# Norm 2's shift and the first low parts move from GpSimd to VectorE, the first gates into a step of their own, the last masks back

## The chip, the cores and the metric

The kernel runs on one core of a Trainium2 chip. The metric is the device time of one execution in microseconds (us). The engines have short names in the profile: PE (TensorE, matrix products and transposes), DVE (VectorE), ACT (ScalarE), POOL (GpSimd), SP (SyncE, which only issues transfers here). PEld is PE's loading of weights.

## What is computed

Two layers over 256 tokens and 256 context tokens of width 1024. Each layer modulates a norm, runs four mixers side by side, adds their output to the residual, norms again, and sends the result through a mixture of 16 experts. What the change touches is the second norm and the experts:

```python
def modulate(h, shift, scale):
    return h * (1.0 + scale) + shift

x = x + gt1 * (jnp.concatenate([ya, yb, ys, yh], axis=-1) @ w_out[l])
h2 = modulate(rms_norm(x, norm2_g[l]), sh2, sc2)
x = x + gt2 * moe(h2, router_w, router_b, moe_w1[l], moe_w3[l], moe_w2[l])
```

`moe` takes the softmax of the 16 router logits, picks the best of four groups of experts by the sum of its two best scores, keeps the two best experts of that group, divides their scores by their sum (the gates), and adds gate times `(silu(h @ w1) * (h @ w3)) @ w2` of these two. Layer 0 does all of this for the context as well; layer 1 for the 256 tokens alone.

## The kernel before

Rows (tokens) lie on the 128 partitions: layer 0 has four tiles of 128 rows in this part, layer 1 two. `wout` multiplies by `w_out`, and for each half of a tile `done` makes the new residual (`yf<-mm,gt`, `yf<-yf,x`). `half` squares and transposes it, `logits` multiplies it by the router's weights, `finish` makes the tile's logits (`lgt`) and the exponentials (`sce`). `norm` writes the tile `x` (it is h2 now): residual times the row's factor (`l21z` and its like, from a few 128x1 operations on DVE) times the scale `a`, plus the shift `sh`. The tile goes to `h2d` in DRAM, by a transfer from SP.

`route` then ranks the scores on DVE: `t<-sce`, `rk`, `og`, `Ab`, then `oh` and `rsrc`, the rows of the first two experts (they have fixed places). `z` is a column of zeros, written at the same point; an operation that takes it as bias can't start earlier. `rri` comes at the end of `route`: it says where each row's entry goes in the table of slots. GpSimd scatters eight times (`sld<-rec,rri`; four in layer 1), and loads the table: `rtab` holds row numbers and gates of all other slots.

The experts run one after another. Their rows are gathered by GpSimd from `h2d` (`xg<-h2d,rsrc` for the first, `xg<-h2d,rtab` later), transposed by PE (`tp<-cst,xg`), and split into a high part and the rest (`ah` on ACT, `al` on DVE). Weights come as 1 MB transfers on SP's queue (`raw<-in_wmoe_dram`), at most three in flight. `split` makes their high part on ACT (`hi<-raw`) and their low part on DVE (`lo<-raw,hi`), 128x1024 at a time, and PE takes three products for each pair: high by high, low by high, high by low (`sc` and `mm` are the PSUM tiles). Small experts (all of layer 1, and those with up to 64 slots in layer 0) run in `expert32` with unsplit weights. Results are multiplied by the gate and scattered to `ybd` in DRAM. In each layer a loop for surplus rows, with a barrier of all engines, stands behind the first two experts (`extras`, L2031); with these inputs it makes no pass. The last expert is added from masks in place of the scatter: `rel` is the row number less the tile's first row, and the masks `ah<-iota_b,rel` compare it with a row of numbers.

The order on each engine is that of the code, as generators are stepped by `moe`, except where a scheduler with a table of costs interleaves. Every operation passes one helper, so the profile gives line 383 for all of them (382 in the changed kernel); they are told apart by their tiles.

Of the kernel before, what the change touches and what calls it, by code (L numbers as in the profile page):

```python
# [15 lines left out]
AF = mybir.ActivationFunctionType  # L16
ALU = mybir.AluOpType
AX = mybir.AxisListType

P = 128  # L20
# [29 lines left out]
KORD = ((4, 5, 6, 7, 2, 3, 0, 1), (0, 1, 6, 7, 4, 5, 2, 3))  # L50
SLOTS = (32, 32)
NPRE = 3
NPP = 3
AHEAD2 = (9, 11)
FLIGHT = 3
STAT = 2
# [333 lines left out]
class Kern:  # L390
# [1165 lines left out]
    def wout(self, l, xsrc):  # L1556
        nc, I = self.nc, self.I
# [9 lines left out]
        for k in KORD[l]:  # L1567
            hi, lo = self.hilo()
# [63 lines left out]
        def norm(i, a):  # L1632
            c = 1 if i < 2 else 0
            h = xt[i]
            last = i == ot[-1]
            for n in range(2):
                s = slice(n * 512, n * 512 + 512)
                nc.vector.scalar_tensor_tensor(h[:, s], self.x2[i][n], rs[i], a2[c][:, s], op0=ALU.mult, op1=ALU.mult)
                if last:
                    (nc.vector if n else nc.gpsimd).tensor_tensor(h[:, s], h[:, s], sh[c][:, s], op=ALU.add)  # L1640
                    nc.sync.dma_start(self.h2d[l][a * P:(a + 1) * P, s], h[:, s])
            if last:
                return
            nc.gpsimd.tensor_tensor(h, h, sh[c], op=ALU.add)
            nc.sync.dma_start(self.h2d[l][a * P:(a + 1) * P, :], h)

        def flush(j):
            i, n, t = later[j]
# [272 lines left out]
    def moe(self, l, route):  # L1921
# [29 lines left out]
        for e in range(NE):  # L1951
            if e == STAT:

                while len(self.pre) < AHEAD2[l]:
                    m, j = USE[self.wi]
                    self.pre.append(self.fetch(source(m)(j)))
                self.extras(l)
            if STAT <= e + 2 < NE:
                for n in both(e + 2):
                    xg[n] = self.gather(l, *sl[n], m=min(P, SLOT[l][e + 2]))  # L1960
            for j in range(2):
                if e or j:
                    next(gens[e])
                if e:
                    next(gens[e - 1], None)
            next(gens[e])
            if e == NE - 1:
                while self.wi < len(USE):
                    self.pre.append(self.fetch(source(USE[self.wi][0])(USE[self.wi][1])))
                self.combine_g2(l)  # L1970
            if e + 1 < NE:
                begin(e + 1)
            next(gens[e])
# [77 lines left out]
    def halves_of(self, wsrc, alone, n):  # L2051

        nc = self.nc
        for j in range(6):
            if not alone:
                raw = self.load(wsrc(j))
            for hf in range(2):
# [5 lines left out]
                        self.splitx(*hl, src[:, q])  # L2063
                        yield hl
                else:
                    hi, lo = self.split(raw[:, c], after=self.zero0 if NPP <= 2 * j + hf < n else None, eng=nc.gpsimd if 2 * j + hf < min(n, NPP) else None)
                    yield hi[:, 0:512], lo[:, 0:512]
                    yield hi[:, 512:1024], lo[:, 512:1024]

    def expert(self, l, wsrc, tiles, m, ahead=0, alone=False):  # L2070
# [50 lines left out]
        for n in range(2):  # L2121
# [5 lines left out]
                    self.mm3(ps[:m], es[i][0][:, t], es[i][1][:, t], hi, lo, k == 0, k == 3)  # L2127
            c = slice(n * 512, n * 512 + 512)
            for i, ps in enumerate(py):
                nc.scalar.activation(ys[i][:m, c], ps[:m], AF.Copy, scale=tiles[i][2][:m])  # L2130
        for y, (_, rows, *_) in zip(ys, tiles):
            self.add_rows(l, y, rows, m)

# [10 lines left out]
    def expert32(self, l, wsrc, tile, m, last=False):  # L2144
# [51 lines left out]
        if G > 1:  # L2196
# [3 lines left out]
                    nc.tensor.matmul(pt[:, o:o + m], lhsT=s[:, k * P:(k + 1) * P], rhs=self.fold, start=True, stop=True)  # L2200
            t = self.act("al", F32)
            nc.scalar.activation(t[:, :4 * m], pt[:, :4 * m], AF.Silu)
            nc.vector.tensor_tensor(h[:, :4 * m], t[:, :4 * m], pt[:, 4 * m:8 * m], op=ALU.mult)
        else:
            nc.vector.tensor_tensor(s1[:m], s1[:m], p3[:m], op=ALU.mult)
            for k in range(4):
# [2 lines left out]
        if last:  # L2209

            self.ohT = self.act("ah", F32R).rearrange("p (a t) -> p a t", t=P)[:m]
            rel = self.s([P, 4], "rel", bufs=1)
            for a in range(NT):
                nc.vector.tensor_scalar(rel[:m, a:a + 1], rows[:m], 1.0 - 128.0 * a, None, op0=ALU.add)
                nc.vector.tensor_scalar(self.ohT[:, a], self.iota_b[:m], rel[:m, a:a + 1], None, op0=ALU.is_equal)
            t = self.ring_tile(F32R)
            yh, yl = self.ylast = t[:m, 0], t[:m, 1]
        yield
# [135 lines left out]
```

## Time and profile before

| | us |
|---|---|
| median of 3 runs | 1307.47 (1305.84 to 1308.94) |
| profiled execution, its own time | 1307.14 |
| its span, first to last instruction | 1305.1 |
| PE, DVE, ACT, POOL busy | 1146.0, 731.1, 529.9, 183.9 |
| granted clock of PE, mean share | 0.931 |

The span is what the views below divide up; the 2.0 us between it and the execution's own time lie outside it. Starts of instructions are counted from the span's begin. Layer 0's second norm and routing take about 360 to 403 us, its experts before the loop 403 to 450; the same in layer 1 is 965 to 1000 and 1000 to 1042.

### The profile page before, as it was taken

The numbers are of one execution on the slowest core, as the hardware profiler recorded it, in microseconds if no ns is written. First come the engines' busy times: TensorE is split into PE (matmuls) and PEld (weight loads), VectorE is DVE, ScalarE is ACT, GpSimd is POOL, SyncE is SP. The second block draws the span as 40 slices with busy tenths as digits, with TensorE's granted clock in tenths as the row PEclk, the third lists the DMA queues.
The fourth block names the chain that finished last, engine by engine and source line by source line (L and its number), as shares of the span: only waits on it lengthen the run. The fifth ranks groups of instructions, "written<-read, shape, count | busy, mean of one in ns | idle before, by whom it ended". The sixth has DMA issues, their size and how long they took to land. (4 is left out here: it accounts for less than half of the span.)

```text
span 1305.1 us, 16882 instructions
## 1 busy us (share of the span) xinstructions
PE 1146.0 (88%) x5789; PEld 724.5 (56%) x5789; DVE 731.1 (56%) x1811; ACT 529.9 (41%) x876; POOL 183.9 (14%) x213
## 2 busy tenths in 40 slices
PE   4999999997966799999898799998884499998885
PEld 2677677765855567655454277684771253533332
DVE  6496579788588564455444659599974110101114
ACT  5222642674324464555434452553831122212222
POOL 0200200100044220211100100100102111211102
PEclk9999999896987799999999899999896789999997
DMA  7763752444817798899995743554477699999961
GB/s 298 261 235 135 257 204 86 177 153 158 350 49 258 238 355 319 313 367 387 384 361 183 279 162 131 201 173 162 149 277 314 242 337 396 365 389 388 414 265 65
DMA packets 62009, 334.05 MB, mean 256 GB/s; under 512 B 12217, under 2 KB 13657, under 8 KB 27104
## 3 DMA queue, kind: packets, MB, share of 16 engines
q1 hardware_dynamic: 51840, 313.44, 63.0%
q0 software_dynamic: 10080, 19.50, 5.8%
q8 instruction: 47, 0.77, 0.2%
q14 instruction: 42, 0.34, 0.1%
HBM read 317.51 MB, written 19.15 MB: 258 GB/s over the span
## 5 line engine op out<-in xcount | busy, mean ns | idle before, releaser
L383 DVE TENSOR_TENSOR lo<-raw,hi 128x1024 fp32r<-128x1024 f32 x169 | 203.5, 1222 | 87.4 <-ACT hi L383 82.9
L383 PE MATMUL sc<-raw,ah 128*64 128x512 f32 (+3 forms) x750 | 216.2, 634 | 12.8 <-SPq L2031 9.5
L383 ACT CAST hi<-raw 128x1024 fp32r<-128x1024 f32 x172 | 175.3, 1047 | 116.5 <-PE mm L383 53.6
L383 PEld LDWEIGHTS sc<-raw,ah 128*64 128x64 f32 (+3 forms) x750 | 62.3, 147 | 113.3 <-issue 99.5
L383 PE MATMUL mm<-hi,ah 128*128 128x512 f32 (+3 forms) x264 | 109.1, 415 | 4.4 <-ACT hi L383 4.3
L383 PE MATMUL mm<-lo,ah 128*128 128x512 f32 (+3 forms) x264 | 107.0, 405 | 1.7 <-DVE lo L383 1.6
L383 PE MATMUL mm<-hi,al 128*128 128x512 f32 (+3 forms) x264 | 105.7, 402 | 0.6 <-DVE al L383 0.6
L383 PE MATMUL mm<-raw,ah 128*64 128x512 f32 (+3 forms) x378 | 100.2, 595 | 1.9 <-DVE ah L383 1.9
L383 PE MATMUL mm<-ah,hi 128*128 128x512 f32 (+1 forms) x224 | 88.4, 399 | 1.1 <-DVE ah L383 0.8
L383 PE MATMUL sc<-hi,ah 128*128 128x512 f32 (+3 forms) x176 | 75.8, 432 | 11.5 <-ACT hi L383 6.8
L383 DVE COPY al<-sc 128x512 f32<-128x512 f32 x21 | 14.5, 690 | 126.8 <-PE sc L383 126.8
L383 PE MATMUL mm<-al,hi 128*128 128x512 f32 (+1 forms) x224 | 83.8, 374 | 0.0
L383 PE MATMUL mm<-ah,lo 128*128 128x512 f32 (+1 forms) x224 | 83.2, 372 | 0.0
L383 PE MATMUL ad<-raw,cT 128*32 128x256 f32 (+1 forms) x512 | 67.7, 530 | 11.3 <-DMA raw<-in_wada_dram 8.5
L383 DVE TENSOR_TENSOR s<-s,mm 64x512 f32<-64x512 f32 (+1 forms) x43 | 29.2, 678 | 85.1 <-ACT s L383 85.1
L383 PE MATMUL sc<-lo,ah 128*128 128x512 f32 (+3 forms) x176 | 73.2, 416 | 2.1 <-DVE lo L383 2.1
L383 PE MATMUL sc<-hi,al 128*128 128x512 f32 (+3 forms) x176 | 72.1, 410 | 0.0
L383 PEld LDWEIGHTS tp<-fold,al 128*128 128x128 f32 x336 | 43.0, 201 | 48.9 <-DVE al L383 23.9
L383 PE MATMUL tp<-fold,al 128*128 128x64 f32 x336 | 46.9, 289 | 23.8 <-DVE al L383 14.9
L383 PEld LDWEIGHTS mm<-hi,ah 128*128 128x128 f32 (+3 forms) x264 | 49.4, 188 | 28.3 <-ACT hi L383 6.4
L383 PEld LDWEIGHTS mm<-raw,ah 128*64 128x64 f32 (+3 forms) x378 | 32.7, 142 | 58.3 <-issue 52.0
L383 ACT ACTIVATE al<-tp 128x256 f32<-128x256 f32 x21 | 8.1, 384 | 130.1 <-PE tp L383 130.1
(432 smaller groups left out, 2037.0 us busy)
## 6 DMA issues: line engine op xcount, KB each, us to landing
raw<-in_wmoe_dram SPq DMA_DIRECT2D x192, 1024.0 KB
raw<-in_wada_dram SPq DMA_DIRECT2D x32, 1024.0 KB
raw<-in_win_dram SPq DMA_DIRECT2D x24, 1024.0 KB
raw<-in_wad_dram SPq DMA_DIRECT2D x16, 1024.0 KB
raw<-in_wout_dram SPq DMA_DIRECT2D x8, 1024.0 KB
x<-in_tok_dram SPq DMA_DIRECT2D x8, 512.0 KB
raw<-ybd SPq DMA_DIRECT2D x6, 512.0 KB
slot<-yf SPq DMA_DIRECT2D x36, 64.0 KB
```

The source lines that it names most:

```text
L383: r = f(*a, **k)
```

## The change

1. `norm`: the shift is added by DVE, half a tile (128x512) right behind the multiply of that half. Before, GpSimd added it, 128x1024 at a time, apart from the last tile of a layer, of which GpSimd added the first half and DVE the second.
2. `halves_of`: in layer 0 the first expert's first three low parts were made on GpSimd, and their high parts on ACT waited for nothing but their weights. Now they are made on DVE like all others, and the first three high parts wait for `z` (`after=self.zero0`).
3. `expert`: with `ahead` (the first expert of layer 0) the two halves of the result are copied out of PSUM without the gate, and a multiply of the whole row by the gate follows in a step of the generator of its own. `moe` has one more step for it.
4. `expert32(last)`: the instructions of `rel` and of the masks are ordered behind the product `h`. Before, the masks' operands alone put them in order.

```diff
-NPP = 3
...
                 nc.vector.scalar_tensor_tensor(h[:, s], self.x2[i][n], rs[i], a2[c][:, s], op0=ALU.mult, op1=ALU.mult)
+                nc.vector.tensor_tensor(h[:, s], h[:, s], sh[c][:, s], op=ALU.add)
                 if last:
-                    (nc.vector if n else nc.gpsimd).tensor_tensor(h[:, s], h[:, s], sh[c][:, s], op=ALU.add)
                     nc.sync.dma_start(self.h2d[l][a * P:(a + 1) * P, s], h[:, s])
-            if last:
-                return
-            nc.gpsimd.tensor_tensor(h, h, sh[c], op=ALU.add)
-            nc.sync.dma_start(self.h2d[l][a * P:(a + 1) * P, :], h)
+            if not last:
+                nc.sync.dma_start(self.h2d[l][a * P:(a + 1) * P, :], h)
...
             next(gens[e])
+            if e:
+                next(gens[e - 1], None)
...
-                    hi, lo = self.split(raw[:, c], after=self.zero0 if NPP <= 2 * j + hf < n else None, eng=nc.gpsimd if 2 * j + hf < min(n, NPP) else None)
+                    hi, lo = self.split(raw[:, c], after=self.zero0 if 2 * j + hf < n else None)
...
-                nc.scalar.activation(ys[i][:m, c], ps[:m], AF.Copy, scale=tiles[i][2][:m])
+                if ahead:
+                    nc.scalar.copy(ys[i][:m, c], ps[:m])
+                else:
+                    nc.scalar.activation(ys[i][:m, c], ps[:m], AF.Copy, scale=tiles[i][2][:m])
+        if ahead:
+
+            yield
+            for y, (_, _, gate) in zip(ys, tiles):
+                nc.scalar.activation(y[:m], y[:m], AF.Copy, scale=gate[:m])
...
-            nc.vector.tensor_tensor(h[:, :4 * m], t[:, :4 * m], pt[:, 4 * m:8 * m], op=ALU.mult)
+            i = nc.vector.tensor_tensor(h[:, :4 * m], t[:, :4 * m], pt[:, 4 * m:8 * m], op=ALU.mult)
...
-            for a in range(NT):
-                nc.vector.tensor_scalar(rel[:m, a:a + 1], rows[:m], 1.0 - 128.0 * a, None, op0=ALU.add)
-                nc.vector.tensor_scalar(self.ohT[:, a], self.iota_b[:m], rel[:m, a:a + 1], None, op0=ALU.is_equal)
+            with self.tc.issue_after(i.ins):
+                for a in range(NT):
+                    nc.vector.tensor_scalar(rel[:m, a:a + 1], rows[:m], 1.0 - 128.0 * a, None, op0=ALU.add)
+                    nc.vector.tensor_scalar(self.ohT[:, a], self.iota_b[:m], rel[:m, a:a + 1], None, op0=ALU.is_equal)
```

The order of DVE's instructions at the end of layer 0's routing, before, around `rri` (`rr` and `rXT` are its last steps, `al_3810` and `al_3819`, the first expert's, stand 18 and 16 rows ahead of it):

```order
L383 TENSOR_REDUCE rXT_3742<-rov_3740 128x4
L383 SCALAR_TENSOR_TENSOR rr_3758<-rXT_3742 128x8
L383 TENSOR_TENSOR lo_3856<-raw_3085,hi_3855 128x1024
L383 SCALAR_TENSOR_TENSOR rr_3758<-rq_3757,rr_3758 128x8
L383 TENSOR_TENSOR lo_3866<-raw_3085,hi_3865 128x1024
L383 TENSOR_SCALAR rri_3764<-rr_3758 128x8
```

And now, on DVE, from ahead of the first `al` (a third low part, `lo_3796`, stands 21 rows higher, behind `z`) and then up to `rri`:

```order
L382 TENSOR_TENSOR lo_3800<-raw_3081,hi_3799 128x1024
L382 TENSOR_REDUCE rXT_3745<-rw_3749 128x4
L382 TENSOR_TENSOR lo_3804<-raw_3083,hi_3803 128x1024
L382 TENSOR_TENSOR rw_3749<-ru_3744,o_773_3689 128x64
L382 TENSOR_TENSOR al_3813<-tp_3807,ah_3812 128x512
```

```order
L382 TENSOR_TENSOR lo_3859<-raw_3085,hi_3858 128x1024
L382 TENSOR_REDUCE rXT_3745<-rov_3743 128x4
L382 TENSOR_TENSOR lo_3869<-raw_3085,hi_3868 128x1024
L382 TENSOR_TENSOR rov_3743<-ru_3744,o_773_3689 128x64
L382 TENSOR_TENSOR lo_3897<-raw_3087,hi_3896 128x1024
L382 TENSOR_REDUCE rXT_3745<-rov_3743 128x4
L382 TENSOR_TENSOR lo_3907<-raw_3087,hi_3906 128x1024
L382 SCALAR_TENSOR_TENSOR rr_3761<-rXT_3745 128x8
L382 SCALAR_TENSOR_TENSOR rr_3761<-rq_3760,rr_3761 128x8
L382 TENSOR_SCALAR rri_3767<-rr_3761 128x8
```

Three low parts have come ahead of the first `al`. Between `z` and `rri` there are now eight (`lo_3848`, not shown, is the fourth), where there were two.

The order of ACT at the end of expert 0, where its result `y` leaves PSUM, before and now (`hi` are the next expert's high parts; the second half's `y` stood two `hi` further down before):

```order
L383 CAST hi_3997<-raw_3270 128x1024
L383 ACTIVATE y_3949<-mm_3950,rtab_3790 128x512
L383 CAST hi_4007<-raw_3270 128x1024
L383 CAST hi_4020<-raw_855_4018 128x1024
```

```order
L382 CAST hi_3997<-raw_3270 128x1024
L382 COPY y_3952<-mm_3953 128x512
L382 CAST hi_4007<-raw_3270 128x1024
L382 CAST hi_4020<-raw_855_4018 128x1024
L382 COPY y_3952<-mm_3975 128x512
L382 CAST hi_4030<-raw_855_4018 128x1024
L382 ACTIVATE y_3952<-y_3952,rtab_3793 128x1024
L382 CAST hi_4074<-raw_866_4072 128x1024
```

The instruction that reads `rtab` has moved behind three more high parts.

The order of DVE at the end of layer 1's routing, before and now (`al<-sc` and `ah` are an `expert32`'s):

```order
L383 TENSOR_SCALAR rri_9064<-rr_9060 128x4
L383 TENSOR_SCALAR rel_10696<-rtab_9078 64x1 x2
L383 COPY al_9124<-sc_9092 128x512
L383 TENSOR_TENSOR ah_9134<-al_9144,tp_9135 128x256
L383 TENSOR_TENSOR s_1996_9154<-s_1996_9154,mm_9149 64x512
```

```order
L382 TENSOR_SCALAR rri_9069<-rr_9065 128x4
L382 COPY al_9129<-sc_9097 128x512
L382 TENSOR_TENSOR ah_9139<-al_9149,tp_9140 128x256
L382 TENSOR_TENSOR s_1996_9159<-s_1996_9159,mm_9154 64x512
```

`rel`, which reads `rtab`, has left this place; it now stands directly ahead of the masks of the last expert, in layer 0 (four) as in layer 1 (two).

## Rows read from the trace of the kernel before

**Rows 1.** The page: the span, and each engine's busy time, share and instructions.

```profile
span 1305.1 us, 16882 instructions
...
PE 1146.0 (88%) x5789; PEld 724.5 (56%) x5789; DVE 731.1 (56%) x1811; ACT 529.9 (41%) x876; POOL 183.9 (14%) x213
```

**Rows 2.** Table by stage: length, engines' busy time (instructions), granted clock, DMA share, GB/s.

```profile
core 0: us, PE busy (x) PEld busy (x) DVE busy (x) ACT busy (x) POOL busy (x), PEclk, DMA share, GB/s
360.00:403.00 43.00, 20.72 (x125) 17.96 (x124) 38.22 (x116) 9.45 (x22) 21.67 (x12) 0.72 0.16 58
403.00:431.00 28.00, 26.53 (x110) 20.79 (x110) 20.46 (x42) 15.68 (x18) 11.45 (x9) 0.89 0.93 351
985.00:1000.00 15.00, 1.84 (x16) 1.45 (x16) 6.23 (x44) 0.50 (x1) 3.96 (x4) 0.50 0.59 234
1060.00:1260.00 200.00, 188.51 (x848) 80.68 (x844) 25.88 (x42) 46.78 (x82) 27.00 (x22) 0.97 1.01 391
```

**Rows 3.** PE's timeline, where it starts again behind each layer's barrier: start, duration, operation, [idle].

```profile
449.63 0.80 PE L383 MATMUL sc<-hi,ah 128*128 128x512 f32 x1 [4.72 <-issue]
...
1042.00 1.98 PE L383 MATMUL sc<-raw,ah 128*64 128x512 f32 x4 [9.50 <-SPq L2031]
```

**Rows 4.** GpSimd's timeline, layer 0's routing; in brackets idle time before <- releaser.

```profile
365.06 2.82 POOL L383 TENSOR_TENSOR x<-x,sh 128x1024 f32<-128x1024 f32 x1 [29.60 <-DVE x L383]
...
373.57 6.97 POOL L383 TENSOR_TENSOR lo<-raw,hi 128x1024 fp32r<-128x1024 f32 x3 [2.67 <-ACT hi L383]
```

**Rows 5.** VectorE's timeline, the same stage.

```profile
363.50 0.74 DVE L383 SCALAR_TENSOR_TENSOR x<-yf,l20z,a 128x512 f32<-128x512 f32 x1
...
364.90 3.53 DVE L383 SCALAR_TENSOR_TENSOR x<-yf,l21z,a 128x512 f32<-128x512 f32 x2
...
369.09 2.36 DVE L383 TENSOR_TENSOR yf<-yf,x 128x512 f32<-128x512 f32 x1
...
376.00 2.27 DVE L383 SCALAR_TENSOR_TENSOR l22u<-l22z,l22h 128x1 f32<-128x1 f32 x1
...
384.98 1.21 DVE L383 TENSOR_TENSOR lo<-raw,hi 128x1024 fp32r<-128x1024 f32 x1
...
393.33 0.68 DVE L383 TENSOR_TENSOR x<-x,sh 128x512 f32<-128x512 f32 x1
```

**Rows 6.** VectorE's timeline, layer 1's routing.

```profile
994.62 0.16 DVE L383 TENSOR_SCALAR z<-tp 128x1 f32<-128x1 f32 x1 [8.31 <-DMA h2d<-x]
```

**Rows 7.** The first gather and what follows: timelines of GpSimd, PE and VectorE.

```profile
398.57 1.11 POOL L383 DMA_INDIRECT xg<-h2d,rsrc  x1 [4.80 <-DVE rcap L383]
...
403.09 1.94 PE L383 MATMUL tp<-cst,xg 128*128 128x128 f32 x8 [5.57 <-DVE wix L383]
...
404.83 0.69 DVE L383 TENSOR_TENSOR al<-tp,ah 128x512 fp32r<-128x512 f32 x1 [0.33 <-ACT ah L383]
```

**Rows 8.** Layer 0 up to the barrier: timelines of GpSimd, ScalarE and PE.

```profile
412.71 1.90 POOL L383 DMA_INDIRECT sld<-rec,rri  x1 [9.95 <-DVE rri L383]
...
424.42 1.27 POOL L383 DMA_INDIRECT sld<-rec,rri  x1 [0.31 <-issue]
...
435.69 1.63 POOL L383 DMA_INDIRECT ybd<-y,rtab  x1 [0.30 <-DMA xg<-h2d,rtab]
...
442.43 1.05 POOL L383 DMA_INDIRECT xg<-h2d,rtab  x1 [5.12 <-PE tp L383]
...
431.64 0.69 ACT L383 ACTIVATE y<-mm,rtab 128x512 f32<-128x512 f32 x1 [5.59 <-DMA rtab<-sld]
...
433.31 0.80 PE L383 MATMUL sc<-hi,ah 128*128 128x512 f32 x1 [3.13 <-ACT hi L383]
...
441.12 1.03 PE L383 MATMUL tp<-cst,xg 128*128 128x128 f32 x8
```

**Rows 9.** Layer 1 up to the barrier: timelines of VectorE and PE.

```profile
1017.57 0.21 DVE L383 TENSOR_SCALAR rel<-rtab 64x1 f32<-64x1 int32 x2 [15.03 <-DMA rtab<-sld]
...
1017.70 0.67 DVE L383 COPY al<-sc 128x512 f32<-128x512 f32 x1
...
1018.42 1.97 PE L383 MATMUL tp<-fold,al 128*128 128x64 f32 x8 [6.99 <-DVE al L383]
```

**Rows 10.** VectorE's timeline, the end of layer 1.

```profile
1278.03 4.34 DVE L383 TENSOR_SCALAR ah<-iota_b,rel 64x128 fp32r<-64x128 bf16 x2
```

## The prediction

> **What bounds the kernel now.** I read the page first, then a table by stage, then each engine's timeline at the two places that the diff touches, with the waits in it. The page gives TensorE (PE) 1146.0 us of a span of 1305.1, VectorE (DVE) 731.1, GpSimd (POOL) 183.9 [rows 1]. The table shows how little that average says here: in layer 0's routing stage, 360 to 403 us, PE is busy 20.72 of 43 us and DVE 38.22; in 403 to 431 PE has 26.53 of 28; in 1060 to 1260 the DMA share is 1.01 [rows 2]. So DVE sets the pace from 360 to 403, and later what happens on it is mostly covered. Does a gain in that stage survive the stages behind it? I take it that it does: in each layer a loop of zero passes ends with a barrier of all engines, behind which PE starts again at 449.63 and at 1042.00 [rows 3]. Up to there the transfers in flight have landed, so the engines start from the same state however early it is, and the stages bound by PE or by DMA behind it move along. What counts is how far each of the two barriers moves.
>
> **Part 1: the shift on DVE, layer 0.** GpSimd's timeline beside DVE's shows a pattern. While GpSimd adds (2.82 us from 365.06) or makes a low part (three, 6.97 us from 373.57) [rows 4], DVE's operations last until GpSimd is through: a pair of multiplies 3.53 us where one takes 0.74, an add 2.36, a 128x1 operation 2.27 [rows 5] where another takes 0.16 [rows 6]. The excess up to the last tile's logits: the pair 3.53 - 1.48 = 2.05; two adds (one shown) 2 x (2.36 - 0.68) = 3.4; three 128x1 operations (one shown) 3 x 2.1 = 6.3; together 11.75. The low part that DVE itself makes there, 1.21 [rows 5], goes to a later place. New on DVE are halves of the shift, of which one is there today, with 0.68 us [rows 5]; six stand ahead of the last logits, 4.1. DVE idles 43 - 38.22 = 4.8 us in this stage [rows 2], in waits for PE or ScalarE (ACT); I let a third of the new work fall into them, 1.4. Net 11.75 + 1.2 - 4.1 + 1.4 = 10.2. Behind the last logits one more stall goes and one more half comes, about even. So the first gather, issued at 398.57, and PE's transposes of its rows at 403.09 [rows 7] come **10.2 us earlier**. Bounds: 7.6, if the low part's 1.2 and the waits' 1.4 give nothing; below nothing, if it isn't GpSimd that stretches DVE (rival F).
>
> The Trainium skill, "SBUF — State Buffer", section "Who interferes with whom", says that a VectorE instruction with two SBUF inputs and a GpSimd instruction that reads SBUF shut each other out for a whole instruction; the 3.53 and 2.36 us agree, and the 2.27 of an operation on one column as well. By it all of the 11.75 goes and rival F is out.
>
> **Part 2: what DVE does instead.** Expert 0's first low parts are now made on DVE, behind the routing, since their high parts wait for its `z`. The order of DVE shows three of them ahead of the first `al`, which ends today at 404.83 + 0.69 = 405.52 with 0.33 of waiting before it [rows 7]; PE wants it for its third product. 3 x 1.2 - 0.3 = 3.3 us. The four high parts on ACT lie between `z` and the gathered rows, inside the 4.5 us that the gather takes to PE (398.57 to 403.09 [rows 7]): nothing; if that cover were gone, they would cost their length. PE's products of expert 0 move by 10.2 - 3.3 = 6.9.
>
> GpSimd's eight scatters wait for `rri`, 9.95 us until 412.71 [rows 8]. `rri` stood behind two low parts and stands behind eight. Six more cost 7.2 if nothing covers them; 3.3 if they fit into DVE's waits for the high parts and only PE's delay counts. I take 6.3, close to the first, as DVE has few gaps there: `rri`, and with it the table, come 10.2 - 6.3 = **3.9 earlier** (bounds 3.0 and 6.9).
>
> **Part 3: the gate in a step of its own.** Today ACT waits 5.59 us for the table at 431.64 with `y<-mm,rtab`, high parts queue behind it, and PE idles 3.13 until 433.31 [rows 8]. Now three more high parts stand ahead of the multiply that needs the table, and PE can go on. Then come transposes of rows gathered by the table, at 441.12 today [rows 8]. The table is there at 431.6 - 3.9 = 427.7, a gather takes 4.5 to PE, and I allow GpSimd 0.5 to begin it: 432.7, 8.4 earlier. GpSimd's last gather ahead of the barrier, 442.43, waits for those transposes, and the barrier opens 7.2 us behind it (449.63) [rows 3, 8]: 441.2 by this chain. The other is `ybd`, 435.69 today [rows 8]; it keeps its distance of 4.0 from the table, comes at 431.8, and needs no more than the 13.9 that it has to the barrier today: 445.7 at the latest. Between the two I take 442.6, nearer to the first, since `ybd` is not the last to be issued: **-7.0** for layer 0, bounds -3.9 (the table's gain alone) and -10.2 (the first gather's).
>
> **Part 4: the masks held back.** In layer 1 two `rel` wait 15.03 us for the table on DVE until 1017.57. The copy `al<-sc` is queued behind them, and PE waits for it 6.99 us, until 1018.42 [rows 9]. With `rel` gone the copy runs when PE's `sc` is done, and PE goes on at 1011.4. The barrier at 1042.00 [rows 3] moves by **-6.5**, with half a us lost on the way; bounds -7.0 and 0 (rival A). At the end `rel` now stands ahead of the masks: two take 0.21 [rows 9], four in layer 0 twice that, and in layer 1 they stand in a place where DVE is stretched (4.34 for two masks at 1278.03 [rows 10]): **+0.6** in all.
>
> Layer 1's adds and stalls I cost at nothing: at 994.62 DVE waits 8.31 us for the transfer of those very rows [rows 6]; without that cover three halves would cost 2.0.
>
> **Sum.** -7.0 - 6.5 + 0.6 = -12.9. The profiled execution took 1307.14 with its span of 1305.1, and the median of the three is 1307.47; the sum is made against 1307.1: **1294.2 us**, a span of about 1292.
>
> **The rivals.** 0.2% (2.6 us) is about what a measurement of this kernel can tell from no change.
>
> A. Layer 1's wait is hidden anyway. PE's 9.50 us of idle time ahead of 1042.00 end with SyncE's queue [rows 3], which carries the weights; if its last transfers end as today, PE only idles longer. Against it: they wait for buffers that PE frees. 1307.1 - 7.0 + 0.6 = 1300.7. Chance 0.12.
>
> B. The low parts eat layer 0's gain: the gather gains only 7.6, and `rri` loses 7.2 of it; table, gather and barrier keep 0.4. -0.4 - 6.5 + 0.6: 1300.8. For it: `rri` is the head of the longest chain to the barrier. 0.12.
>
> C. GpSimd's scatters stretch with a busier DVE. Eight of them fill 412.71 to 425.69, the first with 1.90 us, the last with 1.27 [rows 8]. At 1.90 and a gap of 0.3 each they would fill 17.6 instead of 13.0: the table 4.6 later, layer 0 -2.4: 1298.8. 0.04. The Trainium skill, "SBUF — State Buffer", in its box on the "DVE blocks DMA" trap, says that a transfer issued by GpSimd waits for its descriptors while VectorE runs in a two-port mode; that speaks against work moved to VectorE, and by it the time would be C's. The scatters' lengths here, unequal beside low parts on DVE, leave it open.
>
> D. All of it counts: the gather's 10.2 and the masks' 7.0. 1307.1 - 17.2 + 0.6 = 1290.5. 0.10.
>
> E. Slower, by PE's clock. Where PE runs in pieces, 985 to 1000, the granted clock is 0.50, its 1.2 GHz; in 403 to 431 it is 0.89 [rows 2]. If low parts made one by one break expert 0's products up so that PE stays at 1.2 GHz through them, 26.53 us become 26.53 x 0.89 / 0.50 = 47.2, 20.7 longer: layer 0's barrier comes 20.7 - 10.2 = 10.5 later, and the sum is 10.5 - 6.5 + 0.6 = +4.6: 1311.7. It decides from 18.7 of these 20.7 on (2.6 over). Against it: 110 products in 26.53 us are 0.24 each, six of them to a low part 1.45, more than the 1.2 that DVE takes. 0.08.
>
> F. Something other than GpSimd stretches DVE, and the change doesn't do what it says. Then seven halves (4.8) and the three low parts (3.3) come on top of today's time; with -7.0 + 0.6 that is +1.7: 1308.8, no change by the bound. 0.06.
>
> **How the numbers follow.** My own case has 0.48; its own range is 1291 to 1299.5, layer 0 between -9.5 and -3.9 and layer 1 between -7.0 and -5. From 1289 to 1302.5 lie A to D too; E and F (0.14) and a few ends of the others are left out. Faster: 0.48 + 0.12 + 0.12 + 0.04 + 0.10 = 0.86. Same: F, 0.06. Slower: E, 0.08.
>
> **What would show it.** Right: no DVE operation of one column over 0.5 us and no pair over 1.6 from 361 to 380; the first gather near 388; the scatters from about 408.5; no wait of PE for a high part behind expert 0; the first barrier near 442.6; in layer 1 `al<-sc` without a wait for the table, and the distance between the barriers 6 to 7 us shorter. Wrong: a gather that moved with a barrier that did not (B); a longer idle time ahead of the second barrier (A); a granted clock near 0.5 in expert 0 (E).

## The result, and the profile after

| | before | changed |
|---|---|---|
| median, first comparison | 1306.65 us (4 runs, 1299.51 to 1308.94) | 1289.55 us (4 runs, 1286.50 to 1294.32) |
| ratio, 95% interval | | 0.9889 (0.9856 to 0.9921) |
| median, second comparison | 1307.27 us (11 runs) | 1293.10 us (6 runs) |
| ratio, 95% interval | | 0.9884 (0.9856 to 0.9913) |
| profiled execution, its own time; span | 1307.14; 1305.1 | 1286.50; 1283.3 |

Faster by 1.1 to 1.2%, some 15 us. (The ratios are the recorded ones, with their intervals; the medians by themselves would give 0.987 and 0.989.) The page after, span and busy times, beside [rows 1]:

```profile
span 1283.3 us, 16883 instructions
...
PE 1135.7 (88%) x5789; PEld 717.1 (56%) x5789; DVE 723.3 (56%) x1824; ACT 531.7 (41%) x877; POOL 162.0 (13%) x204
```

GpSimd has lost 21.9 us, DVE 7.8, although DVE has more instructions (1824 for 1811): it does more and waits less inside its instructions. The timeline of DVE in layer 0's routing, beside [rows 5]:

```profile
358.32 0.74 DVE L382 SCALAR_TENSOR_TENSOR x<-yf,l20z,a 128x512 f32<-128x512 f32 x1
...
359.72 0.75 DVE L382 SCALAR_TENSOR_TENSOR x<-yf,l21z,a 128x512 f32<-128x512 f32 x1
...
362.45 0.68 DVE L382 TENSOR_TENSOR yf<-yf,x 128x512 f32<-128x512 f32 x1
...
367.06 0.22 DVE L382 SCALAR_TENSOR_TENSOR l22u<-l22z,l22h 128x1 f32<-128x1 f32 x1
...
382.18 0.16 DVE L382 TENSOR_SCALAR rsrc<-tp 128x2 int32<-128x2 f32 x1 [0.30 <-PE tp L382]
```

Up to `rsrc` no operation is stretched any more: a single multiply takes 0.75, the add 0.68, the operation of one column 0.22 (2.36 and 2.27 before). The next rows are GpSimd, PE, VectorE and ScalarE from the first gather to the barrier, beside [rows 3, 7, 8]:

```profile
383.18 1.11 POOL L382 DMA_INDIRECT xg<-h2d,rsrc  x1 [13.31 <-DVE rcap L382]
...
384.29 1.87 POOL L382 MEMSET xg<- 128x1024 f32 x2
...
387.53 1.94 PE L382 MATMUL tp<-cst,xg 128*128 128x128 f32 x8 [5.39 <-DMA xg<-h2d,rsrc]
...
392.43 0.80 PE L382 MATMUL sc<-hi,al 128*128 128x512 f32 x1 [1.91 <-DVE al L382]
...
397.14 0.39 PE L382 MATMUL sc<-lo,ah 128*128 128x512 f32 x1
...
384.92 1.28 DVE L382 COPY rat<-cst 128x2 f32<-128x2 f32 x1
...
385.34 1.19 DVE L382 TENSOR_TENSOR lo<-raw,hi 128x1024 fp32r<-128x1024 f32 x1
...
402.50 0.17 DVE L382 TENSOR_SCALAR rri<-rr 128x8 int32<-128x8 f32 x1
...
402.95 1.03 POOL L382 DMA_INDIRECT sld<-rec,rri  x1 [15.50 <-DVE rri L382]
...
419.27 0.61 POOL L382 DMA_DIRECT2D rtab<-sld  x1 [3.87 <-DMA sld<-rec,rri]
...
431.55 1.05 POOL L382 DMA_INDIRECT xg<-h2d,rtab  x1 [1.60 <-PE tp L382]
...
423.96 1.15 ACT L382 ACTIVATE y<-y,rtab 128x1024 f32<-128x1024 f32 x1 [6.43 <-DMA rtab<-sld]
...
429.33 1.94 PE L382 MATMUL tp<-cst,xg 128*128 128x128 f32 x8 [7.93 <-DMA xg<-h2d,rtab]
...
437.71 0.66 PE L382 MATMUL sc<-hi,ah 128*128 128x512 f32 x1 [2.15 <-issue]
```

In layer 1, DVE and PE, beside [rows 3, 6, 9], and the masks at the end, beside [rows 10]:

```profile
981.89 0.16 DVE L382 TENSOR_SCALAR z<-tp 128x1 f32<-128x1 f32 x1 [9.21 <-DMA h2d<-x]
...
997.07 0.69 DVE L382 COPY al<-sc 128x512 f32<-128x512 f32 x1 [7.21 <-PE sc L382]
...
997.81 2.00 PE L382 MATMUL tp<-fold,al 128*128 128x64 f32 x16
...
1014.10 1.08 PE L382 MATMUL tp<-cst,xg 64*128 64x64 f32 x8 [6.37 <-DMA xg<-h2d,rtab]
...
1022.36 1.97 PE L382 MATMUL sc<-raw,ah 128*64 128x512 f32 x4 [3.82 <-SPq L2030]
...
1256.88 0.20 DVE L382 TENSOR_SCALAR rel<-rtab 64x1 f32<-64x1 int32 x2
...
1257.05 3.97 DVE L382 TENSOR_SCALAR ah<-iota_b,rel 64x128 fp32r<-64x128 bf16 x2
```

The reader is to see three things. `al<-sc` waits for PE, not for the table; PE goes from one product to the next there (997.81) and waits later, 6.37 us, for rows gathered by the table. In layer 0 PE has no wait for a high part; it now waits 7.93 us for gathered rows at 429.33. And the starts can't be compared as they stand: the stage itself began 5.18 us earlier (358.32 for 363.50 [rows 5]), ahead of any instruction that the change touches. So all places below are counted from DVE's first `x<-yf,l20z` in layer 0, and in layer 1 from `z<-tp`:

| us | gather (POOL) | `rri` (DVE) | table at ACT | transposes (PE) | barrier 1 (PE) | barrier 1 to `z` | `z` to barrier 2 | from there to the end |
|---|---|---|---|---|---|---|---|---|
| before | 35.07 | 48.76 | 68.14 | 77.62 | 86.13 | 544.99 | 47.38 | 263.08 |
| changed | 24.86 | 44.17 | 65.63 | 71.01 | 79.39 | 544.18 | 40.47 | 260.95 |
| difference | -10.21 | -4.59 | -2.51 | -6.61 | **-6.74** | -0.81 | **-6.91** | -2.13 |

With the 5.18 ahead of it all, the row adds up to the spans' difference of 21.8 us: 5.18 + 6.74 + 0.81 + 6.91 + 2.13. The changed kernel profiled again (e10, below) gave barrier 1 at 79.65 and `z` to barrier 2 in 40.51, but began the stage at 363.89 and had a span of 1292.9. So some 13.5 us come back each time, and the 5.18 did not; they are the spread between executions, which reaches 9 us for one kernel. In the fourteen profiles of this document the stage begins between 358.32 and 364.61, and up to there the instructions of all of them are the same, in the same order.

Barrier 1 has a spread of its own: e12 (below) differs from the changed kernel in layer 1 alone, and its first barrier comes at 77.56. Three profiles with the same instructions up to there thus give 77.56, 79.39 and 79.65, and smaller differences than these 2.1 us, between two profiles, say little about it.

Which engine holds barrier 1? It opens when the last one has come to it. In the kernel before that is VectorE, with a low part that ends at 447.76, 1.87 us ahead of PE's restart:

```profile
446.54 1.22 DVE L383 TENSOR_TENSOR lo<-raw,hi 128x1024 fp32r<-128x1024 f32 x1
```

Now it is ScalarE, with a high part that ends at 436.64, 1.07 ahead of the restart, and two low parts stand behind the barrier:

```profile
435.60 1.04 ACT L382 CAST hi<-raw 128x1024 fp32r<-128x1024 f32 x1 [0.69 <-PE sc L382]
...
438.43 2.36 DVE L382 TENSOR_TENSOR lo<-raw,hi 128x1024 fp32r<-128x1024 f32 x2 [2.14 <-issue]
```

From the stage's begin to the barrier VectorE and GpSimd made 24 low parts before, and VectorE makes 22 now. None of the four parts of the change names this; the order of the code came out so.

The second barrier waits for weights. The table by stage for eight microseconds ahead of it, before and then now (the column ahead of the last is the DMA share):

```profile
core 0: us, PE busy (x) PEld busy (x) DVE busy (x) ACT busy (x) POOL busy (x), PEclk, DMA share, GB/s
1015.00:1023.00 8.00, 4.58 (x16) 2.61 (x17) 1.22 (x4) 0.38 (x1) 1.96 (x2) 0.50 0.34 124
```

```profile
1010.00:1018.00 8.00, 3.90 (x16) 1.69 (x16) 0.00 (x0) 0.58 (x1) 0.07 (x1) 0.58 1.02 334
```

Before, the transfers of weights had a hole behind PE's stop at 1011.43: SyncE's queue waited for PE's `sc` products, which had to free the buffers, 9.4 us at the longest; now it is 2.9, and the DMA share stays at 1.0 until 1018. In both kernels the transfers are through 1.4 to 2 us ahead of PE's restart (the share is 0.00 from 1040 before, and from 1021 now). So what came back in layer 1 is the hole in the transfers, and PE's new wait at 1014.10 costs nothing, as the weights move on during it.

### The profile page after: what moved, and what is told of

It is laid out like the page before. It is cut to its first block, busy times and chain, and to the rows that moved or that the text cites. A ratio compares the mean times of both kernels' runs of the same rounds, so it can differ in the third digit from the quotient of the medians.

```text
span 1283.3 us, 16883 instructions
## 1 busy us (share of the span) xinstructions
PE 1135.7 (88%) x5789; PEld 717.1 (56%) x5789; DVE 723.3 (56%) x1824; ACT 531.7 (41%) x877; POOL 162.0 (13%) x204
## 5 line engine op out<-in xcount | busy, mean ns | idle before, releaser
L382 DVE TENSOR_TENSOR lo<-raw,hi 128x1024 fp32r<-128x1024 f32 x172 | 206.6, 1221 | 85.7 <-ACT hi L382 80.1
L382 ACT CAST hi<-raw 128x1024 fp32r<-128x1024 f32 x169 | 172.2, 1047 | 112.6 <-PE mm L382 52.9
L382 PE MATMUL sc<-raw,ah 128*64 128x512 f32 (+3 forms) x750 | 213.3, 628 | 6.2 <-SPq L2030 3.8
L382 PE MATMUL tp<-cst,xg 64*128 64x64 f32 (+4 forms) x264 | 31.4, 261 | 32.9 <-DMA xg<-h2d,rtab 14.3
```

Source lines behind the costliest of these rows:

```text
L382: r = f(*a, **k)
```

## The experiments

All places are counted as in the table above.

**One part at a time.** Each kernel is the one before with one of the four edits of the diff above; e5 has two of them.

e1, the shift alone:

```diff
+                nc.vector.tensor_tensor(h[:, s], h[:, s], sh[c][:, s], op=ALU.add)
...
-            nc.gpsimd.tensor_tensor(h, h, sh[c], op=ALU.add)
```

> Only the shift moves to VectorE; the three first low parts stay on GpSimd. Counted from VectorE's first x<-yf,l20z in layer 0: rsrc came 34.06 us later before, 23.86 with the whole change. Theory (GpSimd's adds stretch VectorE, each for as long as it runs): the pair, two adds and the t<-sce give back about 6.4, seven halves cost 4.7, GpSimd's low parts still cost 6: rsrc at about 32, first barrier 2 us earlier, layer 1 unchanged, time -2 us. Rival (something else stretches VectorE): the halves come on top, rsrc at 38 to 39, time +4.

e4, the low parts alone:

```diff
-                    hi, lo = self.split(raw[:, c], after=self.zero0 if NPP <= 2 * j + hf < n else None, eng=nc.gpsimd if 2 * j + hf < min(n, NPP) else None)
+                    hi, lo = self.split(raw[:, c], after=self.zero0 if 2 * j + hf < n else None)
```

> Only the three low parts move to VectorE, their high parts behind z; the shift stays on GpSimd. Theory: the three stretched 128x1 operations (6.3) and the low part on VectorE (1.2) go: rsrc at 34.06 - 7 = 27; six low parts more ahead of rri take 5 to 6 of it back: rri at 48.76 - 1 = 47.5, first barrier 0 to 1 us earlier, time the same. Rival (the first gather alone decides): barrier 5 us earlier, time -5.

e2, the masks alone:

```diff
+            with self.tc.issue_after(i.ins):
```

> Only the masks are held back. Theory: layer 1's stretch from z to PE behind the second barrier, 47.38 us before and 40.47 with the whole change, falls to about 40.5 by this part alone; layer 0's first barrier (86.13 after the first x<-yf,l20z) does not move, since ScalarE's gated y still waits for the table there; time -6 us. Rival (the barrier's wait hides it, the gain came from elsewhere): 47 stays and the time is the same.

e3, the gate alone:

```diff
+                if ahead:
+                    nc.scalar.copy(ys[i][:m, c], ps[:m])
...
+        if ahead:
+
+            yield
+            for y, (_, _, gate) in zip(ys, tiles):
+                nc.scalar.activation(y[:m], y[:m], AF.Copy, scale=gate[:m])
```

> Only the gate gets its own step. Theory: ScalarE no longer waits for the table at the first y, but VectorE's rel still does, with low parts queued behind it, so PE still stops for a low part within a few us: first barrier within 1 us of 86.13, time the same. Rival (the gate alone held PE): PE runs on to the transposes, barrier 3 to 4 us earlier, time -3.5.

e5, gate and masks together, both edits as above:

> The gate's own step and the masks held back, together; shift and low parts as before. The gate alone put the first barrier at 88.09 us after the first x<-yf,l20z (86.13 before), the masks alone at 86.16. Theory: each alone only passes the wait for the table to the other engine, both together take it off PE's path; PE's transposes, 77.62 before, come 5 behind the table's 68, at 73, and the barrier at 82; layer 1 as with the masks alone (41.7), time -10 us. Rival (the parts only add): barrier at 88, time -4.

e11, the whole change but the gate:

```diff
-                if ahead:
-                    nc.scalar.copy(ys[i][:m, c], ps[:m])
-                else:
-                    nc.scalar.activation(ys[i][:m, c], ps[:m], AF.Copy, scale=tiles[i][2][:m])
+                nc.scalar.activation(ys[i][:m, c], ps[:m], AF.Copy, scale=tiles[i][2][:m])
```

> The whole change without the gate's own step. Theory (ScalarE's gated y holds three high parts back until the table is there, at about 65.5, and only then come 4.6 us of products or more ahead of the transposes): transposes at 74, first barrier at 82 to 83 instead of 79.4, time 3 us more than the whole change. Rival (PE waits for the table's rows in either order): barrier at 79.4, same time.

e10, the changed kernel again, with no edit:

> The changed kernel itself, for its time in the same call. Theory: ratio to before 0.989, first barrier at 79.4, layer 1's stretch from z to the second barrier at 40.5. Rival (part of the first result, 5 us of which stood ahead of any changed instruction, was chance): ratio 0.992 to 0.993 with the same stretches.

What was measured:

| kernel | `rsrc` | `rri` | table at ACT | transposes | barrier 1 | `z` to barrier 2 | ratio (95%) |
|---|---|---|---|---|---|---|---|
| before | 34.06 | 48.76 | 68.14 | 77.62 | 86.13 | 47.38 | 1 |
| e1 shift | 31.25 | 45.91 | 65.00 | 74.51 | 82.80 | 48.42 | 0.9991 (0.9973 to 1.0008) |
| e4 low parts | 27.04 | 47.56 | 65.80 | 74.69 | 83.96 | 47.90 | 1.0011 (0.9991 to 1.0031) |
| e2 masks | 34.04 | 47.11 | 68.24 | 77.66 | 86.16 | 41.69 | 0.9965 (0.9945 to 0.9985) |
| e3 gate | 34.04 | 47.17 | 67.28 | 78.26 | 88.09 | 47.82 | 1.0060 (1.0039 to 1.0082) |
| e5 gate, masks | 34.05 | 47.19 | 69.77 | 75.71 | 85.04 | 40.99 | 0.9926 (0.9902 to 0.9951) |
| e11 all but gate | 23.86 | 44.33 | 62.62 | 71.42 | 80.52 | 40.40 | 0.9888 (0.9857 to 0.9918) |
| e10 all | 23.87 | 42.13 | 65.47 | 70.84 | 79.65 | 40.51 | 0.9884 (0.9856 to 0.9913) |
| e12 all, layer 1's shift as before | 23.86 | 43.75 | 65.14 | 70.18 | 77.56 | 40.69 | 0.9855 (0.9821 to 0.9888) |

e1 and e4 came out as the theory had them at `rsrc` (31.25 for 32, 27.04 for 27), and against the rival of e1, 38. e4's `rri` did as well (47.56 for 47.5): 7 us at the gather, 1.2 at `rri` (and nothing against the 47.1 and 47.2 of kernels whose `rri` has the order of before). That shows the low parts on VectorE taking the gain back. Barrier 1 gained more than `rri` there: 2.2, with 0 to 1 expected. e2 shows the masks to be worth 5.7 us in layer 1 by themselves and nothing at the first barrier, as expected. The hole in layer 1's transfers goes with them: counted in steps of 4 us from 8 us behind `z`, the DMA share falls to 0.29 to 0.32 in the kernel before, e1, e3 and e4, and to no less than 0.95 in e2. e10's interval, up to 0.9913, leaves out its rival's 0.992.

The times of e1 and e4 save nothing that can be seen. For e1 that is still in reach of its 3.3 us, which its layer 1 gives back in part (48.42). e4's interval, 1.2 us less to 4.0 more, leaves its 2.2 out; its profile loses as much between barrier 1 and `z` (547.21), and why is open. With both parts in, e11 saves some 10 us more than e2 (0.9888 and 0.9965), 5.6 of them ahead of barrier 1.

e3 is a miss in sign: nothing was expected, and the first barrier came 2.0 later, the time 0.6%. GpSimd and VectorE behind the table, in e3:

```profile
431.45 6.18 POOL L383 DMA_INDIRECT xg<-h2d,rtab  x1 [2.68 <-DMA rtab<-sld]
...
430.70 0.33 DVE L383 TENSOR_SCALAR rel<-rtab 64x1 f32<-64x1 int32 x4 [4.99 <-DMA rtab<-sld]
...
430.95 5.75 DVE L383 TENSOR_TENSOR lo<-raw,hi 128x1024 fp32r<-128x1024 f32 x5
...
432.21 0.50 PE L383 MATMUL sc<-lo,ah 128*128 128x512 f32 x1 [3.39 <-DVE lo L383]
...
441.75 1.94 PE L383 MATMUL tp<-cst,xg 128*128 128x128 f32 x8 [3.76 <-DMA xg<-h2d,rtab]
```

PE does stop for a low part behind `rel` (3.39 us), as the theory had it. But the gather that it needs next takes GpSimd 6.18 us, for 1.05 in the kernel before, and ends 0.93 us behind five low parts in a row on VectorE (437.63, and 430.95 + 5.75 = 436.70). That delay is long enough for the 2 us that were lost (this barrier, too, opens behind low parts of VectorE), but was not varied by itself (the last section has what all profiles show of it): in the kernel before, five low parts from 433.29 took 6.12 us, with more room between them, and the two instructions of GpSimd beside them 1.75 and 1.63. The time of e3, 1.006, is more than this stretch explains; the rest stays open. e5 undid the loss (85.04), but gave 1.1 at the first barrier where 4 were expected: its table was 1.6 later than before's, and transposes came 5.9 behind it. e11 missed on the other side: its first barrier, 80.52, is 0.9 to 3.0 us behind the three profiles of the whole change (79.65, 79.39, 77.56), and its time is theirs (0.9888 for 0.9884), where 3 us more were expected. ScalarE does wait for the table and PE for ScalarE (5.14 us), but the table came sooner:

```profile
420.78 0.61 POOL L383 DMA_DIRECT2D rtab<-sld  x1 [3.28 <-DMA sld<-rec,rri]
...
422.87 0.69 ACT L383 ACTIVATE y<-mm,rtab 128x512 f32<-128x512 f32 x1 [7.60 <-DMA rtab<-sld]
...
424.54 0.80 PE L383 MATMUL sc<-hi,ah 128*128 128x512 f32 x1 [5.14 <-ACT hi L383]
```

In e11 PE is idle while the table is loaded, and few transfers run; the load takes 2.09 us from GpSimd's 420.78 to ScalarE's 422.87. In the changed kernel it takes 4.69 (419.27 to 423.96). The table by stage for these two stretches, e11 first, then the changed kernel (columns as above; the one ahead of the last is the DMA share):

```profile
420.70:422.90 2.20, 0.00 (x0) 0.00 (x0) 0.00 (x0) 0.03 (x1) 0.61 (x1) 1.00 0.04 8
```

```profile
419.00:424.00 5.00, 2.40 (x11) 1.66 (x9) 0.00 (x0) 0.04 (x1) 0.61 (x1) 1.00 0.81 330
```

A share of 0.04 there and of 0.81 here. In thirteen profiles ScalarE waits for this load: it took 2.00 to 3.57 us at a DMA share of up to 0.44 (six), and 4.57 to 5.09 at 0.62 and more (seven). So this small transfer took longer among the weights; no run varied the share by itself.

At the first barrier the shift alone gives 3.3, the low parts alone 2.2, and gate and masks together (e5) 1.1: 6.6, for 6.74, 6.48 (e10) and 8.57 (e12) of the whole. The gate alone costs 2.0 and the masks alone give 0, so those two do not add up; and each figure is of one profile, with a spread of some 2 us, so that the agreement to a tenth is chance.

**What GpSimd does to VectorE.** Both kernels are the whole change, with work added on GpSimd that nothing reads. e7:

```diff
             if not last:
                 nc.sync.dma_start(self.h2d[l][a * P:(a + 1) * P, :], h)
+                if l == 0:
+                    dum = self.sx([P, 512], "dum", BF16)
+                    for n in range(2):
+                        s = slice(n * 512, n * 512 + 512)
+                        nc.gpsimd.tensor_tensor(dum, h[:, s], sh[c][:, s], op=ALU.add)
```

> The whole change, and behind each of the first three tiles' shifts in layer 0 GpSimd adds tile and shift once more into a scratch tile that nobody reads (two 128x512 adds to bf16 a tile). Theory (a GpSimd instruction that reads SBUF shuts out VectorE's with SBUF inputs): VectorE's operations beside them last until they end, rsrc at 28 instead of 23.85. Rival (VectorE was stretched by something else): rsrc stays at 23.9.

e8, six memsets a tile, which wait for the shift of the tile's second half (`ad`):

```diff
+                    for n in range(6):
+                        k = nc.gpsimd.memset(dum, float(n))
+                        self.tc.add_manual_dep(k.ins, ad.ins.name, mybir.DependencyInfo(mybir.DependencyClass.Sync, mybir.DependencyReason.DATA), reason="start")
```

> The same, but GpSimd writes the scratch tile six times a tile (memset) and reads nothing. Theory: memsets don't read, so VectorE's two-input operations run on, rsrc within 1 us of 23.9. Rival (any GpSimd instruction on SBUF shuts VectorE out): rsrc later by about the time that the memsets take.

These two have a profile each and no timed comparison. GpSimd and VectorE in e7:

```profile
363.97 1.27 POOL L382 TENSOR_TENSOR dum<-x,sh 128x512 bf16<-128x512 f32 x1 [30.85 <-DVE x L382]
...
366.78 3.44 POOL L382 TENSOR_TENSOR dum<-x,sh 128x512 bf16<-128x512 f32 x2 [1.54 <-DVE x L382]
...
370.91 1.26 POOL L382 TENSOR_TENSOR dum<-x,sh 128x512 bf16<-128x512 f32 x1 [0.69 <-DVE l22h L382]
...
363.89 0.69 DVE L382 TENSOR_TENSOR yf<-mm,gt 128x512 f32<-128x512 f32 x1
...
367.16 1.25 DVE L382 TENSOR_TENSOR l2s<-l2q 128x1 f32<-128x1 f32 x1
...
369.10 1.67 DVE L382 TENSOR_TENSOR x<-x,sh 128x512 f32<-128x512 f32 x1
...
371.06 1.14 DVE L382 SCALAR_TENSOR_TENSOR l22u<-l22y,l22h 128x1 f32<-128x1 f32 x1
```

and in e8:

```profile
367.82 6.95 POOL L382 MEMSET dum<- 128x512 bf16 x12 [33.57 <-DVE x L382]
...
368.28 0.15 DVE L382 TENSOR_TENSOR l2s<-l2q 128x1 f32<-128x1 f32 x1
...
369.12 0.69 DVE L382 TENSOR_TENSOR x<-x,sh 128x512 f32<-128x512 f32 x1
...
370.10 0.22 DVE L382 SCALAR_TENSOR_TENSOR l22u<-l22y,l22h 128x1 f32<-128x1 f32 x1
```

With reads, VectorE's sum of two columns takes 1.25 for 0.15, its add 1.67 for 0.69, its one-column operation 1.14 for 0.22, and each gets through only when GpSimd's instruction has ended; `rsrc` comes at 28.36 (28 expected). With 6.95 us of memsets beside the same operations they take 0.15, 0.69 and 0.22, and `rsrc` stands at 23.86. So what stretched these operations of two inputs is shown: GpSimd's instructions that read, not those that only write, nor the stage. It is what the Trainium skill, "SBUF — State Buffer", section "Who interferes with whom", states; the first add of e7 (363.97) stretched nothing, and VectorE's instruction beside it (0.69 at 363.89) has one of its two inputs in PSUM.

**Does the table hold the barrier?** The whole change, with expert 0's low parts from the fifth on ordered behind `rri` (e6), then the same with PE's transposes held in their place as well (e9):

```diff
-                    hi, lo = self.split(raw[:, c], after=self.zero0 if 2 * j + hf < n else None)
+                    if n and 2 * j + hf >= 4:
+                        with self.tc.issue_after(self.rri.ins):
+                            hi, lo = self.split(raw[:, c])
+                    else:
+                        hi, lo = self.split(raw[:, c], after=self.zero0 if 2 * j + hf < n else None)
```

> The whole change, and expert 0's low parts from the fifth on are ordered behind rri. Theory (those low parts ahead of rri hold up the table, and the table holds up PE's transposes): rri at 38 instead of 44.17, ScalarE has the table at 60 instead of 65.6, transposes at 65.5 instead of 71.0, first barrier at 74 instead of 79.4; 5 us less than the whole change, ratio to before 0.985. Rival (PE then waits for low parts, or weights on their way set the barrier): transposes earlier, barrier at 79, time as with the whole change, ratio 0.989.

```diff
+            self.pin = l == 0 and e == 2
...
+        pin = self.pin and self.last_mm
...
+                    if pin:
+                        tc.add_manual_dep(i.ins, pin.ins.name, mybir.DependencyInfo(mybir.DependencyClass.NoSync, mybir.DependencyReason.DATA), reason="in this order")
```

> The whole change with expert 0's low parts from the fifth on behind rri, as in the run before, but PE's transposes of the table's rows are held in the place that they have with the whole change (the run before had four of them ahead of expert 0's products, where PE waited 13.71 us for the rows). VectorE differs in four low parts, PE and ScalarE not at all. Theory (table late, transposes late, barrier late): rri at 37.7 after the first x<-yf,l20z, table at 59, transposes at 63.5 to 64 instead of 71.0 (PE is done with the products ahead of them at 63.1), first barrier at 72 instead of 79.4; 7 us less than the whole change, ratio to before 0.984. Rival (weights on their way or ybd set the barrier): transposes at 64, barrier at 77 to 79, time within 2 us of the whole change.

| kernel | `rri` | table at ACT | transposes | barrier 1 | ratio (95%) |
|---|---|---|---|---|---|
| e6 | 37.67 | 71.84 | 63.66 | 84.09 | 0.9945 (0.9925 to 0.9964) |
| e9 | 37.67 | 59.82 | 67.41 | 75.87 | 0.9860 (0.9834 to 0.9887) |

(In e6 ScalarE comes to the table late; GpSimd had it at 58.89 at the latest.) e6 tells nothing of the theory but `rri`: with `rri` earlier in its order, the scheduler put four transposes of the table's rows ahead of expert 0's last products, and PE stood there:

```profile
425.76 1.09 PE L382 MATMUL tp<-cst,xg 128*128 128x128 f32 x4 [13.71 <-DMA xg<-h2d,rtab]
```

In e9 `rri` and the table came as expected (37.67, 59.82), the table 5.3 to 5.8 us ahead of the three profiles of the same layer 0. The transposes came 2.8 to 3.6 ahead of them, and barrier 1 1.7 (e12) to 3.8 (e10), where the theory had 7 and the rival 0 to 2. Its gather and PE's wait, and the table by stage with the changed kernel's for the same step:

```profile
420.35 1.06 POOL L382 DMA_INDIRECT xg<-h2d,rtab  x1 [4.91 <-DMA rtab<-sld]
...
427.25 1.94 PE L382 MATMUL tp<-cst,xg 128*128 128x128 f32 x8 [4.30 <-DMA xg<-h2d,rtab]
```

```profile
420.30:427.30 7.00, 2.70 (x13) 1.95 (x12) 4.76 (x5) 4.76 (x6) 4.69 (x3) 0.89 0.99 361
```

```profile
424.60:429.40 4.80, 0.07 (x1) 0.10 (x2) 3.31 (x3) 4.76 (x6) 4.14 (x3) 0.50 0.44 137
```

The gather takes 6.90 us to PE (420.35 to 427.25) at a DMA share of 0.99, and 4.68 in the changed kernel (424.65 to 429.33) at 0.44: sooner, it runs among the weights. That is 2.2 of the 3.5 that the transposes miss (67.41 for 63.5 to 64), and 0.8 is the table's (59.82 for 59). So the table does hold the transposes, but what is gained at it is only half kept there, and how much of it reaches the barrier lies between 1.7 and 3.8; the rival isn't out for that last step. e7 goes the other way: with `rsrc` 4.5 later its table came 4.3 to 4.8 later (69.94) and barrier 1 4.3 to 6.4 later (83.91), so a delay at the head does reach the barrier. The median is 1287.29 beside 1293.10 for e10 in the same comparison, and the intervals, 0.9834 to 0.9887 and 0.9856 to 0.9913, overlap: that e9 beats the changed kernel is not shown for the time.

**Layer 1's shift.** e12 is the whole change with layer 1's shift back on GpSimd:

```diff
-                nc.vector.tensor_tensor(h[:, s], h[:, s], sh[c][:, s], op=ALU.add)
+                if l == 0 or n and last:
+                    nc.vector.tensor_tensor(h[:, s], h[:, s], sh[c][:, s], op=ALU.add)
+                elif last:
+                    nc.gpsimd.tensor_tensor(h[:, s], h[:, s], sh[c][:, s], op=ALU.add)
...
+            if l and not last:
+                nc.gpsimd.tensor_tensor(h, h, sh[c], op=ALU.add)
```

> The whole change, but in layer 1 GpSimd adds the shift as before. Theory (the wait for the rows' transfer behind ten weights on SyncE's queue hides what VectorE does there): z and all that follows as with the whole change, time the same within 2 us. Rival (layer 1's shift is part of the gain): z 1 to 2 us later, counted from the first barrier, time 2 us more.

Ratio 0.9855 (0.9821 to 0.9888), barrier 1 to `z` 543.07 for 544.18 and 547.80 in the two profiles of the whole change, `z` to barrier 2 40.69. No loss can be seen; the rival is out, as far as executions that differ by 2 us and more in that long stretch can tell.

## Why the prediction was right

- **The bound and the barriers.** From barrier 1 to layer 1's `z` the two kernels differ by 0.8 us, less than two profiles of the changed one do (544.18, 547.80). What is gained ahead of a barrier moved along, as the prediction took it; as the two profiles differ by 3.6 us, it is the times that show it, for the whole change (e10) and not for e4. That transfers have landed at the barriers holds: the DMA share is 0.00 from 448 to 449 and from 1040 to 1042 in the kernel before.
- **Part 1.** -10.2 was forecast at the first gather and -10.21 came. Its two causes are shown apart by e1 and e4 (2.81 and 7.02 at `rsrc`), and the mechanism by e7 and e8. Rival F is out.
- **Part 2.** Three low parts were to make `al` 3.3 us late; PE's third product waited 1.91 us for it (392.43). The first of the three (385.34) lies beside a stretch of VectorE that is there in any case, a copy of two columns that takes 1.28 us at 384.92 beside GpSimd's memset, and costs next to nothing. So that product came 8.3 us earlier, for 6.9 forecast. `rri` came 4.59 earlier for 3.9 forecast; kernels with the same VectorE order there differ by 1.6 to 2 us at this place (48.76 and 47.17 in before and e3, 44.17 and 42.13 in the two profiles of the change).
- **Part 3.** -7.0 was forecast for barrier 1, -6.74 and -6.48 were measured (-8.57 in e12), but not by the way that was forecast. The table was to keep `rri`'s gain, -3.9, and kept 2.51: its own load took 4.69 us in place of 2.25 (429.39 to 431.64 before), at a DMA share of 0.81 beside it, for 0.47 before (429.0 to 431.6). The transposes were to gain 8.4 and gained 6.61. And the path to the barrier was misread: the -7.0 was chosen between GpSimd's last gather and `ybd`, but the barrier opened behind a low part of VectorE before, and opens behind a high part of ScalarE now (446.54 and 435.60 above). From the transposes' start to the end of PE's last product takes 2.45 us more now, as PE comes from a wait of 7.93 at its lower clock (granted 0.50 from 429.3 to 434.4; 1.00 before, from 441.1 to 444.9). From there to PE's restart it takes 2.57 less (2.15 for 4.72), with two low parts behind the barrier. 6.61 - 2.45 + 2.57 = 6.73: that these two terms cancel is luck. The gate, which the part is named for, gives 0.9 to 3.0 us of it by e11, and nothing in the time, once the masks are out of the way.
- **Part 4.** -6.5 was forecast and -6.91 measured; by e2, the part alone gives 5.7 in that stretch. PE's 6.99 us of waiting are gone, and rival A with them, by the reason that the prediction gave against A: the queue's last transfers wait for buffers that PE frees. The barrier follows these transfers, not PE's own time: the idle time ahead of it fell from 9.50 to 3.82 us, and 6.37 came up at 1014.10, for rows that the table gives. The +0.6 at the layers' ends can't be seen: `rel` costs 0.20 ahead of layer 1's masks, and the masks took 3.97 for 4.34.
- **The clock.** Rival E did not happen. PE is at the lower of its two levels around the wait at the third product (granted clock 0.51 from 389.3 to 397.1, 0.63 us a product) and at the higher from 397.14 on (1.00 to 402.3, 0.39 us). In the kernel before it began expert 0 in the same way, with 0.50 from 403.0 to 409.3 and 1.00 behind that.
- **Rivals B, C and D.** The low parts did not eat the gain (B): table and barrier kept 2.51 and 6.74. The scatters did not stretch (C): eight of them fill 12.45 us, from 402.95 to 415.40, for 12.98 before, beside more low parts; the rule cited there is about two-port modes, and no run shows the moved work to use one. D's time, 1290.5, is as near to the medians as the forecast's 1294.2, but its reason, a barrier 1 that keeps the gather's 10.2, did not come: 6.5 to 8.6.
- **Size.** 1294.2 was forecast, 12.9 less; 15 less came by the ratios, some 13.5 of it in the two stretches. The 5.18 us ahead of any changed instruction, in the first profile of the change, are in neither the forecast nor the second profile: the begin of this stage differs by 6.3 us among profiles whose instructions up to there are the same.

## What to carry to other kernels

A transfer of work from an idle engine to a busy one can be a gain, when the idle engine's instructions stand in the busy one's way: add up what the busy engine's instructions last beyond their like while the other one runs, and set that against the work moved. When an instruction that waits for late data is moved off an engine's queue, look which engine then waits for the same data; here neither of the two moves alone gave anything ahead of the first barrier. What a chain gains at its head can be lost in part further down: here a load and a gather that came sooner ran among the weights and took longer. And a barrier opens behind whatever comes to it last: look which engine or which transfer that is, before the change and after it.

## What the runs showed of the hardware

A gather issued by GpSimd, which reads its row numbers from SBUF, took 6.18 us beside five low parts in a row on VectorE (each with two SBUF inputs) in e3, and 1.05 in the kernel before; scatters issued while low parts run take between 0.98 and 2.03 us there. The fourteen profiles bear the low parts out as the cause. 90 gathers in them begin while a low part is running. 84 of these end 0.81 to 0.93 us behind the end of that low part, whether 0.15 or 1.13 us of it were left, and so take 0.96 to 2.00 us; five began within 0.03 us of their low part and took 1.05 to 1.06; the last is e3's, which ended 0.93 us behind the fifth low part. Gathers with no low part beside them take 0.95 to 1.12. The 78 scatters into the table (`sld`) that begin while a low part runs end 0.85 to 0.97 us behind its end. So VectorE can hold up GpSimd's transfers without any of the two-port operations that the Trainium skill, "SBUF — State Buffer", in its box on the "DVE blocks DMA" trap, names. No run varied it by itself; why one gather was held by five low parts and others by one, and whether the gather's reading or its descriptors waited, stays open.
